# Softmax division on GpSimd and ScalarE, rotation read from PSUM, and the keys' factors on GpSimd in a four-layer encoder

## The chip, the cores and the metric

The kernel runs on one core of a Trainium2 chip. A core has a matrix engine (TensorE, PE in the profile), three engines for elementwise work (VectorE = DVE, ScalarE = ACT, GpSimd = POOL) and a queue that issues DMAs (SyncE = SP). PE, DVE and ACT can reach PSUM, the small memory into which PE writes; POOL here only works on SBUF. Each engine executes its own instructions strictly in order and waits on semaphores for the others. The metric is the time of one execution in microseconds (us); lower is better.

## The reference: what is computed

Four residual layers, `x <- x + Mixer(RMSNorm(x))`, on 512 tokens of width 1024, in float32: layer 0 and layer 3 are gated short convolutions (A), layer 1 is sparse attention (B), layer 2 is latent attention (C). All attention is softmax attention with a chunk-causal mask over 16 heads. The parts that the change touches:

```python
# B: q, k are normalised per head, then rotated
q = rope(rmsnorm(q.reshape(bsz, seq, B_HEADS, B_HEAD_DIM), q_norm), positions)
k = rope(rmsnorm(k.reshape(bsz, seq, B_HEADS, B_HEAD_DIM), k_norm), positions)
...
logits = jnp.einsum("qhd,qkhd->qhk", q_b, k_sel).astype(jnp.float32) * scale
p = jax.nn.softmax(logits, axis=-1)
return jnp.einsum("qhk,qkhd->qhd", p, v_sel)
...
# C: k is a nope part per head and a rotary part shared by all heads
k = jnp.concatenate([k_nope, jnp.broadcast_to(kr[:, :, None, :], ...)], axis=-1)
q = rmsnorm(q, q_norm)
k = rmsnorm(k, k_norm)
q = jnp.concatenate([q[..., :C_NOPE], rope(q[..., C_NOPE:], positions)], axis=-1)
```

Rotation of a vector with halves x1, x2 gives `[x1*cos - x2*sin, x2*cos + x1*sin]`. In B each query keeps only the 128 keys with the highest index scores.

## The kernel before

**Matmuls.** A float32 product is made of three passes, high*high, high*low and low*high (`products`, L272; `side_by_side`, L279). Weights come in by DMA as `raw` (L136). `convert` (L139) splits them: ACT writes the rounded high part `whi` (L153), POOL the rest `wlo = raw - whi` (L155). Four buffers each of `whi` and `wlo` stand between this and PE, so every weight that PE multiplies has passed POOL's queue.

**Order.** The program is written as Python generators, and a list scheduler with a simulated timeline fixes the order of each engine's instructions when the program is built. On the chip that order is rigid: an instruction that waits holds back all that stand behind it on its engine.

**Layer A** (`layer_a`) is eight groups of projections and an output projection, with the elementwise mixer on DVE, ACT and POOL beside it.

**Layer B** (`layer_b`). `select` (L754) computes the index scores and finds the top 128 keys with 16 rounds of MAX8 and MATCH_REPLACE8 on DVE for each of three blocks of queries. Woven into it by `weave` are `gate_steps` (gate projections `pz`, finished by `half_silu`, L409, whose first DVE instruction is `zr`, L412) and the projections of the head groups 0 and 1. `project` (L841) makes q, k and v of one group of four heads. In `query_key` (L796) ACT copies each finished PSUM bank to the tile `qk` (L802) and its squares to `qk2` (L804), DVE sums the squares (L805), POOL makes the norm factors with small instructions, among them the power (L269). Keys are multiplied by their factor on DVE (L824). Then `rotate` (L529) makes `ropea = x*C` on POOL (L534), `ropeb` = the other half times T in two DVE instructions (L538), and the sum on DVE (L540). `to_features` (L545) lets PE transpose the result through a bank (L550), and ACT and DVE write it back.

**Attention** (`attention`, L585) serves B and C. Two heads (e = 0, 1) are taken together and cut into chunks of query blocks, with 128+256, 384 and 512 keys. For a chunk `scores` runs the score matmuls, a DVE instruction that masks, scales and finds the minimum (L620), and the exponential on ACT with its sum (L623). `normalise` (L627) takes the reciprocal of the sums and multiplies p by it, both on DVE (L631, L633). `turn` transposes p on PE (L642) and copies it back (ACT L648, sometimes DVE L646), `mix` multiplies with the values (L663). Scores run four chunks ahead of `turn`, and normalise three ahead. A `Filler` puts the remaining projections between the chunks: in B groups 2 and 3, in C groups 1 to 3. These projections have two PSUM banks (tag `pj`).

**Layer C** (`layer_c`). `keys_values` (L991) makes keys and values of four heads, one block of 128 tokens at a time; POOL squares the keys (L1001), DVE sums, POOL makes the factors, and DVE multiplies the nope part and the shared rotary part with them (L1012, L1013). `queries` (L963) copies each bank (ACT L969), squares it (POOL L971), sums (DVE L972), multiplies the nope part by the gains (DVE L975), and rotates the rest. Both end in `to_features`. Before the attention starts, group 0 is projected and two gate steps run.

## Time and profile before

| | |
|---|---|
| runs before | median 1107.57 us of 3 (1105.38 to 1112.42) |
| the profiled execution | 1104.68 us, of which its span (first to last instruction of the program) is 1102.9 us |
| mean granted TensorE clock in it | 0.995 |
| instructions | 16243 |
| stages, from the timeline | layer A to about 250 us, B's index, selection and groups 0 and 1 to about 400, B's attention to about 550, C's latents to about 636, C's group 0 to about 675, C's attention to about 850, the second layer A to the end |

The profile is one execution. A "busy" share is the time in which an engine executed something. The view of groups by line gives, for all instructions of one source line, engine and shape: their count, the busy time together, the mean of one in ns, and then how long the engine stood idle just before them and what ended that idle time. The view of waits sums that idle time by waiting line and by the line it waited for. The view by windows gives, for each stretch of time, the busy time of each engine in us, with the granted clock. The timeline lists instructions with start, duration and, in brackets, the idle time before.

### The profile page before, as it was taken

How to read it: one execution, taken by the hardware profiler on the slowest of the kernel's cores; microseconds unless marked ns; L12 is line 12 of the kernel's file. 1: busy time of each engine (PE TensorE's matmuls, PEld its weight loads, DVE VectorE, ACT ScalarE, POOL GpSimd, SP SyncE). 2: the span in 40 equal slices, each digit the busy share in tenths (PEclk: the TensorE clock that was granted, in tenths of full speed). 3: DMA queues.
4: the chain of work that ended last, by engine and by line, in shares of the span. 5: the costliest groups of instructions: out<-in, count | busy, mean ns of one | idle time of the engine just before them, and what ended most of it. 6: DMA issues, size and time to landing. Idle time of an engine off the chain costs nothing.

```text
span 1102.9 us, 16243 instructions
## 1 busy us (share of the span) xinstructions
PE 1069.5 (97%) x6044; PEld 884.2 (80%) x6044; DVE 636.3 (58%) x1311; ACT 481.8 (44%) x1001; POOL 595.9 (54%) x516
## 2 busy tenths in 40 slices
PE   9999999999997989999999998999989999999998
PEld 7888888897896978888688776676767888888887
DVE  7783243346699998666723266775873474234321
ACT  6343233343443435655544445655563433232331
POOL 5655555756446665353175587263713666555552
PEclk9999999999998999999999999999999999999999
DMA  6333332323221211111022222011111333322332
GB/s 221 96 96 99 100 98 86 94 72 115 77 77 59 78 58 59 39 59 58 20 84 94 67 72 63 17 42 39 59 39 33 101 90 102 96 96 96 96 101 91
DMA packets 26575, 86.44 MB, mean 78 GB/s; under 512 B 3328, under 2 KB 4224, under 8 KB 26496
## 3 DMA queue, kind: packets, MB, share of 16 engines
q1 hardware_dynamic: 26352, 85.36, 24.4%
q8 instruction: 47, 0.77, 0.3%
q14 instruction: 32, 0.26, 0.1%
q10 hardware_dynamic: 144, 0.05, 0.0%
HBM read 83.30 MB, written 2.10 MB: 77 GB/s over the span
## 4 chain that ended last, share of the span: by engine, by line
PE 83%; DVE 11%; ACT 2%; issue 2%; DMA 1%; POOL 1%; SPq 0%; ACTq 0%; DVEq 0%; POOLq 0%
PE pa L276 10%; PE pa L275 10%; PE pa L274 10%; PE po L274 5%; PE po L275 5%; PE po L276 5%; PE o L663 4%; PE s L1038 3%; PE pt L642 3%; DVE ropeb L538 2%; PE pz L274 2%; PE pz L275 2%; PE pz L276 2%; PE tr L550 2%; PE s L283 2%
## 5 line engine op out<-in xcount | busy, mean ns | idle before, releaser
L155 POOL TENSOR_TENSOR wlo<-raw,whi 128x512 fp32r<-128x512 f32 (+4 forms) x315 | 405.2, 1293 | 329.8 <-ACT whi L153 320.8
L153 ACT ACTIVATE whi<-raw 128x512 fp32r<-128x512 f32 (+4 forms) x319 | 195.4, 616 | 366.8 <-PE pa L275 162.4
L275 PE MATMUL pa<-xl,whi 128*128 128x512 f32 x512 | 199.2, 389 | 0.0
L274 PE MATMUL pa<-xh,whi 128*128 128x512 f32 x512 | 198.6, 390 | 0.0
L276 PE MATMUL pa<-xh,wlo 128*128 128x512 f32 x512 | 197.4, 389 | 0.2 <-POOL wlo L155 0.2
L276 PEld LDWEIGHTS pa<-xh,wlo 128*128 128x128 f32 x512 | 96.0, 188 | 20.7 <-POOL wlo L155 0.6
L274 PEld LDWEIGHTS pa<-xh,whi 128*128 128x128 f32 x512 | 96.3, 188 | 20.1 <-ACT xh L346 0.2
L275 PEld LDWEIGHTS pa<-xl,whi 128*128 128x128 f32 x512 | 96.1, 188 | 19.9
L623 ACT ACTIVATE p<-p,mn 128x128 f32<-128x128 f32 (+3 forms) x128 | 71.1, 557 | 43.3 <-DVE mn L620 43.0
L447 DVE TENSOR_TENSOR cg<-pa,R 128x512 f32<-128x512 f32 x16 | 11.1, 691 | 130.2 <-PE pa L276 129.0
L663 PE MATMUL o<-pt,v 128*64 128x128 f32 x640 | 59.0, 283 | 3.6 <-ACT pt L648 2.0
L620 DVE CUSTOM_DVE_ANT_0 p<-s,cmask,qs 128x128 f32<-128x128 f32 (+2 forms) x80 | 38.2, 506 | 38.3 <-PE s L1038 31.7
L663 PEld LDWEIGHTS o<-pt,v 128*64 128x64 f32 x640 | 39.6, 136 | 19.3 <-issue 8.2
L642 PE MATMUL pt<-ident,p 128*128 128x128 f32 x320 | 50.5, 279 | 4.6 <-DVE p L633 3.3
L642 PEld LDWEIGHTS pt<-ident,p 128*128 128x128 f32 x320 | 36.4, 141 | 19.5 <-issue 13.9
L274 PE MATMUL po<-xh,whi 128*128 128x512 f32 x128 | 50.5, 394 | 1.1 <-ACT qT L111 1.1
L276 PE MATMUL pz<-xh,wlo 128*128 128x512 f32 x128 | 51.5, 403 | 0.0
L347 DVE SCALAR_TENSOR_TENSOR xl<-x,gains,xh 128x512 fp32r<-128x512 f32 x32 | 42.2, 1348 | 15.8 <-ACT xh L346 15.4
L423 DVE TENSOR_TENSOR x<-po,x 128x512 f32<-128x512 f32 x24 | 16.2, 689 | 60.6 <-PE po L276 60.6
L274 PE MATMUL pz<-xh,whi 128*128 128x512 f32 x128 | 51.0, 398 | 0.0
L275 PE MATMUL pz<-xl,whi 128*128 128x512 f32 x128 | 50.7, 396 | 0.0
L269 POOL TENSOR_TENSOR y<-mean,minus_half 128x16 f32<-128x16 f32 (+1 forms) x18 | 49.6, 2757 | 1.3
(241 smaller groups left out, 2506.7 us busy)
## 6 DMA issues: line engine op xcount, KB each, us to landing
raw<-in_a_in SPq DMA_DIRECT2D x63, 512.0 KB, 3.9
raw<-in_a_out SPq DMA_DIRECT2D x16, 512.0 KB, 3.9
raw<-in_b_z SPq DMA_DIRECT2D x8, 512.0 KB, 3.5
raw<-in_b_q SPq DMA_DIRECT2D x8, 512.0 KB, 3.4
raw<-in_b_k SPq DMA_DIRECT2D x8, 512.0 KB, 3.5
raw<-in_b_v SPq DMA_DIRECT2D x8, 512.0 KB, 3.4
raw<-in_b_out SPq DMA_DIRECT2D x8, 512.0 KB, 4.0
raw<-in_c_z SPq DMA_DIRECT2D x8, 512.0 KB, 3.6
```

The source lines that it names most:

```text
L153: act_e.activation(hi, raw[:, j:j + m], AF.Copy)
L155: e.tensor_tensor(out=lo, in0=raw[:, j:j + m], in1=hi.bitcast(F32), op=OP.subtract)
L269: pool.tensor_tensor(out=y, in0=m, in1=minus_half[:, :n], op=OP.pow)
L274: nc.tensor.matmul(o, l[0], r[0], start=first, stop=False)
L275: nc.tensor.matmul(o, l[0], r[1], start=False, stop=False)
L276: nc.tensor.matmul(o, l[1], r[0], start=False, stop=last)
L347: dve.scalar_tensor_tensor(lo, X[k], g, hi.bitcast(F32), op0=OP.mult, op1=OP.subtract)
L620: dve.tensor_tensor_reduce(out=p[:, w], in0=banks[e][:, w], in1=j["masks"](t), scale=j["qs"](e, t), scalar=-GONE, op0=OP.add, op1=OP.min, ...
L623: act_e.activation(p[:, w], p[:, w], AF.Exp, bias=mn[e][:, i:i + 1], scale=-1.0, accum_out=sm[e][:, i:i + 1])
L642: pe.transpose(b[:, i:i + P], p[:, i:i + P], ident)
L663: pe.matmul(o[64 * e:64 * e + 64, t * P:(t + 1) * P], j["v"](e, kb), x[e][:, i:i + P], start=t == 0, stop=t == NT - 1 and kb == t)
L1038: pe.matmul(o, sets[g]["q"][2 * i + e][:96, t * P:(t + 1) * P], sets[g]["k"][2 * i + e][:96, :(t + 1) * P], start=True, stop=True)
```

## The change

Four edits.

1. `normalise`: the reciprocal is taken once for both heads of a chunk pair, from one common tile of sums, and the multiplication moves from DVE: for head 0 it is a POOL tensor_scalar, for head 1 an ACT Copy with a per-partition scale.
2. `rotate` takes an optional PSUM bank. With it, the two `ropeb` instructions read the bank instead of the SBUF copy, and the final sum is on POOL instead of DVE. In B's `query_key` the rotation is now called for each bank as it is finished, ahead of the norm factors; in C's `queries` likewise.
3. The keys' factors: B's multiplication (L824 before) and C's two (L1012, L1013 before) move from DVE to POOL. In B the factor is now applied behind the rotation.
4. C's `queries`: the squares are made by ACT straight from the bank (before by POOL from the copy), ACT's copy is cut to the rotary part (4 x 32 columns instead of 384), and the nope part is multiplied by the gains on DVE straight from the bank.

The rotation of the index (idx, key) and of C's shared key keeps its old form.

```diff
-    def rotate(o, x, C, T):
+    def rotate(o, x, C, T, bank=None):
...
-            dve.tensor_tensor(pb[:, :, :, i], x[:, :, :, 1 - i],
+            dve.tensor_tensor(pb[:, :, :, i], (x if bank is None else bank)[:, :, :, 1 - i],
                                     T[:, :, None, i].to_broadcast([P, A, B, half]), op=OP.mult)
-        dve.tensor_tensor(o.rearrange("p a b i j -> p a b (i j)"), pa,
-                                pb.rearrange("p a b i j -> p a b (i j)"), op=OP.add)
+        e = dve if bank is None else pool
+        e.tensor_tensor(out=o.rearrange("p a b i j -> p a b (i j)"), in0=pa,
+                        in1=pb.rearrange("p a b i j -> p a b (i j)"), op=OP.add)
...
-            sm = [tiny("sum", n, tag="small") for _ in range(2)]
+            sm = tiny("sum", 2 * n, tag="small")
...
-                                     accum_out=sm[e][:, i:i + 1])
-                stage[c + e] = p, sm[e]
+                                     accum_out=sm[:, e * n + i:e * n + i + 1])
+                stage[c + e] = p, sm
...
         def normalise(c):
-            ts = chunks[c][2]
+            e, ts = chunks[c][1:3]
             p, sm = stage.pop(c)
-            rc = tiny("rc", len(ts), tag="small")
-            dve.reciprocal(rc, sm)
+            if e == 0:
+                rc = tiny("rc", 2 * len(ts), tag="small")
+                dve.reciprocal(rc, sm)
+                factors[c] = factors[c + 1] = rc
+            rc = factors.pop(c)[:, e * len(ts):(e + 1) * len(ts)]
             for i, (t, w) in enumerate(parts(ts)):
-                dve.tensor_scalar(p[:, w], p[:, w], rc[:, i:i + 1], None, op0=OP.mult)
+                if e == 0:
+                    pool.tensor_scalar(p[:, w], p[:, w], rc[:, i:i + 1], None, op0=OP.mult)
+                else:
+                    act_e.activation(p[:, w], p[:, w], AF.Copy, scale=rc[:, i:i + 1])
...
                 raw.append(x)
+                x5, b5 = (y.rearrange("p t (h i j) -> p t h i j", h=4, i=2)
+                          for y in (x, b.rearrange("p (t c) -> p t c", c=256)))
+                C, T = (tab[:, 2 * i:2 * i + 2] for tab in (tq if which == "q" else tk))
+                rotate(x5, x5, C, T, b5)
...
-                    dve.tensor_tensor(x3, x3, f[:, 8 * i:8 * i + 8, None].to_broadcast([P, 8, 64]), op=OP.mult)
-                x5 = x.rearrange("p t (h i j) -> p t h i j", h=4, i=2)
-                C, T = (tab[:, 2 * i:2 * i + 2] for tab in (tq if which == "q" else tk))
-                rotate(x5, x5, C, T)
+                    pool.tensor_tensor(out=x3, in0=x3, in1=f[:, 8 * i:8 * i + 8, None].to_broadcast([P, 8, 64]),
+                                       op=OP.mult)
...
-                act_e.activation(x, b[:, :384], AF.Copy)
                 q = tile_of("rp", "qk2", (P, 384))
-                pool.tensor_tensor(out=q, in0=x, in1=x, op=OP.mult)
+                act_e.activation(q, b[:, :384], AF.Square)
...
-                x = x.rearrange("p (h d) -> p h d", d=96)
-                dve.tensor_tensor(x[:, :, :64], x[:, :, :64], gqk[:, None].to_broadcast([P, 4, 64]), op=OP.mult)
-                x5 = x[:, :, 64:].rearrange("p (a h) (i j) -> p a h i j", a=1, i=2)
-                rotate(x5, x5, *(tab[:, t:t + 1] for tab in tq))
+                x, b = (y.rearrange("p (h d) -> p h d", d=96) for y in (x, b[:, :384]))
+                act_e.activation(x[:, :, 64:], b[:, :, 64:], AF.Copy)
+                dve.tensor_tensor(x[:, :, :64], b[:, :, :64], gqk[:, None].to_broadcast([P, 4, 64]), op=OP.mult)
+                x5, b5 = (y[:, :, 64:].rearrange("p (a h) (i j) -> p a h i j", a=1, i=2) for y in (x, b))
+                rotate(x5, x5, *(tab[:, t:t + 1] for tab in tq), b5)
...
-                dve.tensor_tensor(x[:, :, :64], x[:, :, :64], yt.to_broadcast([P, 4, 64]), op=OP.mult)
-                dve.tensor_tensor(x[:, :, 64:], krr[:, t, None].to_broadcast([P, 4, 32]),
-                                        yt.to_broadcast([P, 4, 32]), op=OP.mult)
+                pool.tensor_tensor(out=x[:, :, :64], in0=x[:, :, :64], in1=yt.to_broadcast([P, 4, 64]), op=OP.mult)
+                pool.tensor_tensor(out=x[:, :, 64:], in0=krr[:, t, None].to_broadcast([P, 4, 32]),
+                                   in1=yt.to_broadcast([P, 4, 32]), op=OP.mult)
```

More of the change, by code (lines that the diff above doesn't have):

```diff
@@ L595, in attention @@
                 chunks.append(c + (j["fill"][0] + (j["fill"][1] - j["fill"][0]) * (i + 1) / len(mine),))
-        stage, soft, wide, outs = {}, {}, {}, {}
+        stage, soft, wide, outs, factors = {}, {}, {}, {}, {}
         def parts(ts):
```

## The prediction

> **What bounds the kernel now.** I read the engines' shares first, then their course over time, the waits of PE, the windows of the stages that lose PE time, and the timeline around the longest wait.
>
> ```profile
> PE 1069.5 (97%) x6044; PEld 884.2 (80%) x6044; DVE 636.3 (58%) x1311; ACT 481.8 (44%) x1001; POOL 595.9 (54%) x516
> ...
> DVE  7783243346699998666723266775873474234321
> ...
> PEclk9999999999998999999999999999999999999999
> ```
>
> PE is busy 97% of the span. All that other engines can give back is the remaining 33.4 us and a little clock. DVE is full only in slices 11 to 14, some 300 to 410 us: the selection in layer B, where PEclk also dips once.
>
> ```profile
> PE pq L274 <- DVE zr L412: 5.9, 1, 5.9
> PE tr L550 <- DVE kk L1013: 3.5, 3, 1.6
> PE pt L642 <- DVE p L633: 3.3, 3, 1.5
> PE tr L550 <- DVE qk L540: 2.5, 4, 1.6
> ...
> PE pt L274 <- DVE zr L412: 1.3, 1, 1.3
> ...
> PE pt L642 <- DVE rc L631: 1.2, 1, 1.2
> ...
> PE pa L276 <- POOL wlo L155: 0.2, 1, 0.2
> ```
>
> These are PE's waits: us in total, times, longest. Nearly all that ends them is a DVE instruction that the change moves, or one that stood behind such an instruction: 17.7 us in the first six rows. POOL, by contrast, costs PE 0.2 us.
>
> ```profile
> core 0: us, PE busy (x) PEld busy (x) DVE busy (x) ACT busy (x) POOL busy (x), PEclk, DMA share, GB/s
> ...
> 325.00:350.00 25.00, 19.10 (x103) 15.69 (x102) 22.86 (x41) 7.01 (x13) 16.27 (x14) 0.86 0.24 85
> ...
> 450.00:475.00 25.00, 25.00 (x222) 21.69 (x219) 16.18 (x51) 13.84 (x38) 12.96 (x11) 1.00 0.13 43
> ...
> 650.00:675.00 25.00, 21.78 (x110) 17.25 (x109) 17.95 (x32) 12.14 (x25) 20.70 (x22) 1.00 0.20 61
> 675.00:700.00 25.00, 22.38 (x123) 17.39 (x122) 20.87 (x65) 14.47 (x38) 19.49 (x23) 0.93 0.17 51
> 700.00:725.00 25.00, 24.40 (x162) 17.20 (x161) 16.68 (x62) 18.30 (x53) 2.75 (x6) 1.00 0.00 1
> 725.00:750.00 25.00, 25.00 (x138) 20.19 (x137) 20.16 (x55) 12.23 (x30) 19.53 (x20) 1.00 0.15 46
> ```
>
> The stages differ. At 325 DVE is the limit and PE loses 5.9 us. In the middle of B's attention (450) PE is busy throughout, so that relief of DVE is worth nothing there. In C's keys (650 to 700) PE loses 5.8 us, and POOL is the busiest engine after PE: 40.2 of 50 us.
>
> ```profile
> 335.27 3.46 DVE L824 TENSOR_TENSOR qk<-qk,hf 128x512 f32<-128x512 f32 x2 [1.90 <-POOL hf L819]
> ...
> 339.12 4.15 DVE L538 TENSOR_TENSOR ropeb<-qk,table 128x256 f32<-128x256 f32 x4
> ...
> 343.72 0.67 DVE L412 SCALAR_TENSOR_TENSOR zr<-pz,R 128x512 f32<-128x512 f32 x1
> ...
> 344.45 0.58 PE L274 MATMUL pq<-whi,xh 128*128 128x256 f32 x1 [5.90 <-DVE zr L412]
> ...
> 345.47 0.41 PE L275 MATMUL pq<-wlo,xh 128*128 128x256 f32 x1
> 345.69 1.05 PE L550 MATMUL tr<-ident,qk 128*128 128x128 f32 x4
> ...
> 348.83 0.28 PE L276 MATMUL pq<-whi,xl 128*128 128x256 f32 x1
> ```
>
> This is the longest wait. DVE waits 1.90 us for the keys' factor, then applies it and rotates for 7.6 us; `zr`, which frees the bank that PE needs, stands behind. After the wait PE runs at half clock for a while (0.41 us a matmul, 0.28 later).
>
> **The change part by part.** Rows for the costs:
>
> ```profile
> L633 DVE TENSOR_SCALAR p<-p,rc 128x128 f32<-128x128 f32 (+3 forms) x128 | 49.5, 431 | 0.5
> L538 DVE TENSOR_TENSOR ropeb<-qk,table 128x256 f32<-128x256 f32 x32 | 27.5, 909 | 1.7 <-ACT qk L802 1.7
> L540 DVE TENSOR_TENSOR qk<-ropea,ropeb 128x512 f32<-128x512 f32 (+1 forms) x32 | 22.2, 695 | 0.4 <-POOL ropea L534 0.4
> L824 DVE TENSOR_TENSOR qk<-qk,hf 128x512 f32<-128x512 f32 x8 | 8.4, 1091 | 2.8 <-POOL hf L819 2.8
> L1012 DVE TENSOR_TENSOR kk<-kk,y 128x256 f32<-128x256 f32 x16 | 11.9, 741 | 0.0
> L1013 DVE TENSOR_TENSOR kk<-krr,y 128x128 f32<-128x128 f32 x16 | 10.2, 636 | 0.0
> L155 POOL TENSOR_TENSOR wlo<-raw,whi 128x512 fp32r<-128x512 f32 (+4 forms) x315 | 405.2, 1293 | 329.8 <-ACT whi L153 320.8 <-PE po L276 4.3 <-PE po L275 2.1
> L971 POOL TENSOR_TENSOR qk<-qk 128x384 f32<-128x384 f32 x16 | 13.9, 869 | 7.6 <-DVE qk L540 7.5
> L1001 POOL TENSOR_TENSOR qk<-kk 128x256 f32<-128x256 f32 x16 | 10.0, 630 | 43.5 <-ACT kk L998 41.2 <-ACT pt L648 2.0 <-DVE ropeb L538 0.3
> L534 POOL TENSOR_TENSOR ropea<-qk,ti 128x128 f32<-128x128 f32 x16 | 8.7, 544 | 0.0
> L346 ACT ACTIVATE xh<-x,gains 128x512 fp32r<-128x512 f32 x32 | 22.4, 712 | 4.4 <-DVE x L423 4.0 <-DMA x<-in_x 0.2
> L836 ACT ACTIVATE v<-pv,rtok 128x256 f32<-128x256 f32 x16 | 6.4, 474 | 5.7 <-PE pv L276 4.9 <-PE o L663 0.7
> 407.93 0.74 DVE L538 TENSOR_TENSOR ropeb<-qk,table 128x256 f32<-128x256 f32 x2
> 408.01 1.79 POOL L155 TENSOR_TENSOR wlo<-raw,whi 128x512 fp32r<-128x512 f32 x1 [3.68 <-ACT whi L153]
> ```
>
> DVE loses 49.5 (division), 22.2 (rotary sums), 8.4 and 22.1 (keys' factors): 102 us. The two `ropeb` of B take 0.37 us each when POOL rests (the 407.93 row), 0.91 on average and 1.04 in the 339.12 row. Read from PSUM I take 0.4: 32 x 0.5 = 16 us less. In all some 118 of 636 us leave.
>
> POOL gains. The division of head 0 is 64 instructions, 16 each of 128, 256, 384 and 512 elements. No POOL row has a one-input multiply of this size, so I bound it: above by two-input rows, 16 x (0.54 + 0.63 + 0.87 + 1.29) = 53 us; below by DVE's own mean, 64 x 0.43 = 28 us. I take 40, the middle, since one operand less must be read but the engine is the slower one. Sums: 16 x 1.29 + 16 x 0.54 = 29 us. Factors: 8 x 1.29 + 16 x (0.63 + 0.54) = 29 us. The squares that leave: 13.9. Net +84 (72 to 97) on 596 us. Over the whole span that fits; by stage see the second rival.
>
> ACT gains the division of head 1, 16 x (0.36 + 0.47 + 0.59 + 0.71) = 34 us (256 and 512 from rows, the others on their line), and in C 16 narrow copies of 0.36, beside the square that replaces the wide copy: 40 us on 482. Hidden: 700:725 is its fullest window here, and 6.7 of 25 us are free.
>
> No DMA is added or moved. SP's loads go on when `wlo` has consumed `raw`, so they are late only if POOL is; that belongs to the second rival.
>
> Now what lies on PE's path.
>
> 1. The 5.9 us wait and its half clock. The factor, the sums and most of `ropeb` leave DVE, so `zr` can run when its matmuls end. Gain 5.9 us, and a part of the half clock: 0.86 over 25 us means 7 us at half speed; it ended between the 345.47 and 348.83 rows, so 1.0 to 4.4 us of it were work, at a loss of half. I take 1.6 us: 7.5 us together. Late next: the POOL chain for the same keys, power, factor, two multiplies of 1.29. PE transposed these keys at 345.69 and the factor was there at 335.2, so POOL has 10 us for 2.6.
> 2. End of selection: `qk` L540 and `p` L633, 2.5 + 3.3 us. Of these I take 3.0, since the transposes then wait for POOL's sum and division instead.
> 3. C's keys: waits of 3.5 for `kk`, 1.3 for `zr` behind them, and the clock of 0.93 (1.7 us): 6.5. A group's eight factors take 4 x (0.74 + 0.64) = 5.5 us on DVE; on POOL 4 x (0.63 + 0.54) = 4.7 us, behind the power and ahead of conversions that PE needs next. I take half, 3.5.
> 4. Against it: at the ends of both attentions nothing covers the way exponential, reciprocal, division, transpose. The head-0 division now waits for both exponentials (one more ACT instruction, up to 0.7 us) and takes up to 1.29 us instead of 0.43: +0.5 each, 1 us. Inside the attentions it is hidden by the three chunks that lie between division and transpose.
> 5. Against it: banks. PE got a bank back after ACT's two reads; now DVE's `ropeb` reads it too, behind whatever stands in DVE's queue. Bounds: zero (DVE reads beside ACT), and one instruction ahead of it of the 0.7 us of L540's row for each of 32 banks, 22 us. I take 1 us, near zero, because PE was fully busy with other work in the 450 row and the long waits of DVE are what disappears.
>
> Sum: -7.5 - 3.0 - 3.5 + 1 + 1 = -12.0. From the profiled execution's 1104.68 us that is 1092.7. The median of the runs shown is 2.9 us above that execution; I add about half: 1094.
>
> The Trainium skill's page "SBUF — State Buffer", section "Who interferes with whom", says that a DVE instruction with two SBUF inputs contends with a GpSimd one that reads SBUF, one holding the other off entirely, and that a DVE instruction with at most one SBUF input doesn't. The 407.93 and 408.01 rows agree: DVE came first and kept 0.37 us, POOL took 1.79 instead of 1.29. By that rule the reads from PSUM cost 0.4 us however busy POOL is, as I took.
>
> **The rivals.**
>
> *Hidden anyway* (chance 0.24). The scheduler lays out all queues anew, and every wait that goes is replaced by another. For it: in the 450 row PE is full already, and for none of the 17.7 us does the trace show what would be late next. Against it: the 5.9 us wait has one evident cause. Gain 0 to 5 us: 1100 to 1108.
>
> *POOL becomes the bound in C* (chance 0.18), ending on the other side. In 650:700 POOL has 40.2 of 50 us. Two groups add 2 x 4.7 (factors) + 8 x 0.54 (sums) - 8 x 0.87 (squares) = 6.7, and the first pair's division up to 3.3: 50.2 of 50. C's attention, 675 to 850, has eight pairs of heads, so 25 us carry up to 3.8 us of division: in 725:750 that makes 19.5 + 4.7 + 2.2 - 3.5 + 3.8 = 26.7 of 25, and I take the last group as alike. As PE takes all weights through POOL, each overrun, with the 9.8 and 5.5 us in which POOL now idles for its inputs, falls on PE: up to 10 + 2 x 7.2 = 24 us, less the 7.5 of step 1: 1123 with the same 1.3 on top; at half of the 24, 1111. It decides when PE's waits for `wlo`, now 0.2 us, pass 12 us. Against it: with 28 instead of 53 us for the division the overruns vanish, and in 700:725 POOL has room. The Trainium skill's "GPSIMD Engine Reference", section "Engine selection", advises against elementwise work on GpSimd: two-input work about half VectorE's speed, one input near line rate. The 1.29 us for 512 elements agrees with the first; for the second no run here has a row.
>
> *All of it goes* (chance 0.1). The six rows' 17.7 us with both clock dips, and shorter bubbles around them: 22 to 26 us, 1080 to 1085.
>
> **How the numbers follow.** The forecast has 0.48, its own range 1087 to 1101. About 1% (11 us) is what a measurement tells from no change: faster means under 1096.5, slower over 1118.6. Seven tenths of the forecast and all of the third rival lie under it: 0.34 + 0.10 = 0.44. Of the POOL case somewhat over half lies above: 0.10. The rest, 0.46, is within 1%. The range leaves out half of the last rival and a good half of the POOL case, 0.15 in all: 1083 to 1116.
>
> **What would show it.** Right: no wait of several us at `zr` near 340, PEclk without a dip there; L538 near 0.4 us; POOL near 680 us and DVE near 520. Step 3 is right if `kk` waits shrink without waits for `wlo`. Wrong: PE waiting for POOL's p, kk, qk or `wlo`, POOL's one-input multiply above 1.3 us for 512 elements, or PE waiting on banks for `ropeb`.

## The result, and the profile after

| | before | after |
|---|---|---|
| median of the runs compared (us) | 1109.2 (1105.38 to 1112.42) | 1082.38 (1082.1 to 1082.77) |
| ratio after / before | | 0.976, 95% interval 0.9725 to 0.9794 |
| profiled execution (us) / its span | 1104.68 / 1102.9 | 1082.3 / 1080.5 |
| mean granted clock in it | 0.995 | 0.999 |

The change makes the kernel 2.4% faster, 22.4 us between the two profiled executions, where the prediction had 12.0. The medians differ by 26.8: the profiled execution of before was faster than each of the four. Both numbers are used below, each beside its own kind: medians with medians, profiles with profiles.

The page of after, engines and their course:

```profile
PE 1061.9 (98%) x6044; PEld 881.5 (82%) x6044; DVE 520.4 (48%) x1063; ACT 514.0 (48%) x1081; POOL 693.3 (64%) x636
...
DVE  7784234345588964444423244443552463344221
...
POOL 5656555666387898586375589695934765555552
PEclk9999999999999999999999999999999999999999
```

DVE is full in one slice instead of four, the dip of PEclk at slice 12 is gone, and POOL has gained 97 us and is full in four slices. PE's own balance: its idle time in the span fell from 33.4 to 18.6 us, and the busy time of the same 6044 matmuls by 7.6. PE's waits after, in us in total, times, longest:

```profile
PE pt L274 <- DVE ropeb L539: 1.9, 2, 1.2
PE pt L651 <- ACT pt L657: 1.8, 4, 0.9
PE tr L552 <- DVE key L746: 1.5, 1, 1.5
PE o L672 <- ACT pt L657: 1.4, 4, 0.7
...
PE pt L651 <- POOL p L640: 0.9, 2, 0.5
...
PE pz L276 <- POOL wlo L155: 0.4, 1, 0.4
...
PE pa L276 <- POOL wlo L155: 0.3, 1, 0.3
```

All six rows of 17.7 us are gone, and nothing of their size stands in their place. The windows of after at two of the stages discussed, and at POOL's fullest (columns as in the prediction):

```profile
325.00:350.00 25.00, 25.00 (x164) 21.55 (x163) 22.23 (x46) 10.36 (x19) 18.92 (x16) 1.00 0.24 85
375.00:400.00 25.00, 24.60 (x204) 22.42 (x202) 18.66 (x49) 15.49 (x38) 24.66 (x24) 1.00 0.26 85
650.00:675.00 25.00, 23.69 (x133) 19.32 (x131) 10.52 (x36) 18.64 (x49) 24.29 (x33) 1.00 0.17 53
675.00:700.00 25.00, 23.98 (x179) 18.13 (x178) 11.40 (x43) 20.46 (x56) 17.78 (x21) 1.00 0.15 43
```

At 325 PE runs 164 matmuls where it ran 103. POOL is 97 to 99% busy in the second and third rows, and PE still waits for `wlo` only 0.7 us in the whole run.

Where the 22.4 us come from is read off the timelines, at marks that every variant has: the last DVE instruction of the selection that makes a mask, the first matmul of C's latents (the end of B), and the end of the program. In the profiles:

| | selection done | end of B | end |
|---|---|---|---|
| before | 412.19 | 590.39 | 1102.89 |
| after, less before | -16.82 | -11.98 | -22.42 |

So B gives 12.0 us and C 10.4. The prediction's own terms are -9.0 for B (steps 1 and 2, half of 4, and 5) and -3.0 for C. The -16.8 at the mask isn't all gain: the window of after from 300 us to there holds 733 matmuls,

```profile
300.00:395.40 95.40, 95.00 (x733) 88.05 (x733) 84.66 (x202) 45.61 (x93) 81.03 (x69) 1.00 0.24 80
```

where that of before (shown below) holds 770. Some work has moved behind the mask: from there to the end of B, after takes 183.0 us where before took 178.2. A part of these 4.8 us has another cause, the split division, which is taken up below.

### The profile page after: what moved, and what is told of

It reads as the page before. It is cut to its first block, busy times and chain, and to the rows that moved or that the text cites. A ratio compares the mean times of both kernels' runs of the same rounds, so it can differ in the third digit from the quotient of the medians.

```text
span 1080.5 us, 16178 instructions
## 1 busy us (share of the span) xinstructions
PE 1061.9 (98%) x6044; PEld 881.5 (82%) x6044; DVE 520.4 (48%) x1063; ACT 514.0 (48%) x1081; POOL 693.3 (64%) x636
## 4 chain that ended last, share of the span: by engine, by line
PE 91%; DVE 3%; ACT 3%; issue 1%; POOL 1%; DMA 1%; SPq 0%; DVEq 0%; POOLq 0%; ACTq 0%
PE pa L276 10%; PE pa L275 10%; PE pa L274 10%; PE po L274 5%; PE po L275 5%; PE po L276 5%; PE o L672 4%; PE pt L651 3%; PE s L1049 3%; PE pz L276 2%; PE pz L274 2%; PE pz L275 2%; PE tr L552 2%; PE s L283 2%; PE pk L274 2%; PE pq L274 2%
## 5 line engine op out<-in xcount | busy, mean ns | idle before, releaser
L640 POOL TENSOR_SCALAR p<-p,rc 128x128 f32<-128x128 f32 (+1 forms) x64 | 70.3, 1105 | 55.4 <-DVE rc L635 50.1
L672 PE MATMUL o<-pt,v 128*64 128x128 f32 x640 | 56.6, 283 | 1.8 <-ACT pt L657 1.4
L275 PE MATMUL po<-xl,whi 128*128 128x512 f32 x128 | 50.3, 393 | 0.0
L275 PE MATMUL po<-glo,whi 128*128 128x512 f32 x128 | 49.8, 389 | 0.0
```

The lines of the kernel that those rows point to most:

```text
L275: nc.tensor.matmul(o, l[0], r[1], start=False, stop=False)
L640: pool.tensor_scalar(p[:, w], p[:, w], rc[:, i:i + 1], None, op0=OP.mult)
L672: pe.matmul(o[64 * e:64 * e + 64, t * P:(t + 1) * P], j["v"](e, kb), x[e][:, i:i + P], start=t == 0, stop=t == NT - 1 and kb == t)
```

## The experiments

The prediction's theory was that `zr` is freed because the keys' factor and the sums leave DVE. Its rival is that the rotation does it: asked for at each bank and not behind the factor, and read from the bank. Times are medians; ratios are to runs of before taken beside them.

### Each edit alone

`only_division` has edit 1, `only_rotation` edits 2 and 4 (with the key's factor still on DVE), `only_factors` edit 3. Cores of the three diffs against before, in this order:

```diff
-                dve.tensor_scalar(p[:, w], p[:, w], rc[:, i:i + 1], None, op0=OP.mult)
+                if e == 0:
+                    pool.tensor_scalar(p[:, w], p[:, w], rc[:, i:i + 1], None, op0=OP.mult)
+                else:
+                    act_e.activation(p[:, w], p[:, w], AF.Copy, scale=rc[:, i:i + 1])
...
-            dve.tensor_tensor(pb[:, :, :, i], x[:, :, :, 1 - i],
+            dve.tensor_tensor(pb[:, :, :, i], (x if bank is None else bank)[:, :, :, 1 - i],
...
+        e = dve if bank is None else pool
...
-                    dve.tensor_tensor(x3, x3, f[:, 8 * i:8 * i + 8, None].to_broadcast([P, 8, 64]), op=OP.mult)
+                    pool.tensor_tensor(out=x3, in0=x3, in1=f[:, 8 * i:8 * i + 8, None].to_broadcast([P, 8, 64]),
+                                       op=OP.mult)
```

> Edit 1 alone on the kernel before. Theory A (each edit gives what it takes from DVE in the stage where DVE was late): selection in B hardly moves (mask finished at 412 us before, 395 after; here 409 to 412), and the 5.9 us wait of PE for zr stays, since the keys' factor and ropeb still stand ahead of it on DVE; B's attention neutral or 2 us longer; C's attention, from its first score matmul to its last value matmul, falls from 168.4 us to about 163, since a chunk's division no longer stands between other DVE work. Total 5 to 8 us faster than before. Rival B (the division only moved a wait to POOL, whose one-input multiply takes 1.57 us for 512 elements): C's attention stays at 167 to 170 us and the total within 3 us of before.

> Edits 2 and 4 alone on the kernel before (rotation from the bank with its sum on POOL, C's squares on ACT; division and keys' factors stay on DVE). Theory A: the two ropeb pairs of 0.9 us become 0.41 and run early, so the selection ends 6 to 10 us earlier than before (412.2 us), and the 5.9 us wait shrinks, though the factor of 2 x 1.1 us or more and its wait for POOL stay ahead of zr. C's keys and attention change by less than 2 us, since kk stays on DVE. Total 7 to 11 us faster. Rival B (any one part that thins DVE's queue takes away the same long wait): 12 us or more in the selection alone, so that the parts add up to much more than the whole.

> Edit 3 alone on the kernel before (keys' factors of B and C on POOL; rotation and division stay on DVE). Theory A: DVE no longer waits for the factor with zr behind it, so the 5.9 us wait and the half clock go (7.5 us), and C's waits for kk (3.5 us, of which 2.3 in its attention's first 25 us) go too: 3 us in C. Selection ends at about 404 us. Total 8 to 12 us faster. Rival B (the factor on POOL delays the rotation behind it, ropea being on POOL too, and the conversions): selection gains under 4 us and the total is under 5 us.

| | us | ratio (95%) |
|---|---|---|
| only_division | 1102.06 | 0.9942 (0.9923 to 0.9961) |
| only_rotation | 1081.68 | 0.9764 (0.9736 to 0.9792) |
| only_factors | 1109.37 | 1.0013 (0.9996 to 1.003) |

The rotation alone is as fast as the whole change, where 7 to 11 us were expected of it. The factors alone, on which step 1 was built, do nothing, where 8 to 12 us were expected. Only the division came out about as expected. The DVE timeline of `only_factors` at the long wait says why:

```profile
338.29 2.65 DVE L538 TENSOR_TENSOR ropeb<-qk,table 128x256 f32<-128x256 f32 x2 [2.43 <-POOL qk L824]
...
341.40 2.35 DVE L538 TENSOR_TENSOR ropeb<-qk,table 128x256 f32<-128x256 f32 x2
343.68 0.68 DVE L412 SCALAR_TENSOR_TENSOR zr<-pz,R 128x512 f32<-128x512 f32 x1
```

DVE no longer multiplies by the factor, but it stands for 2.43 us until POOL has, because the rotation is still behind the factor; and `zr`, behind the rotation, starts at 343.68, where before it was 343.72. PE's wait stays:

```profile
PE pq L274 <- DVE zr L412: 5.1, 1, 5.1
```

In `only_rotation`, where DVE still multiplies:

```profile
335.74 0.69 DVE L412 SCALAR_TENSOR_TENSOR zr<-pz,R 128x512 f32<-128x512 f32 x1 [2.25 <-PE pz L276]
...
338.26 2.37 DVE L830 TENSOR_TENSOR qk<-qk,hf 128x512 f32<-128x512 f32 x2
```

`zr` now waits for its own matmuls and runs as soon as they end; the factor comes after it. What freed `zr` is that the rotation left the place between the factor and `zr`, not that the factor left DVE. `early_from_copy`, in the next section, is the plain test of this.

### The rotation, place by place and step by step

`rotation_in_b` makes the rotation's edit in B's `query_key` only, `rotation_in_c` in C's `queries` only (with edit 4). `early_from_copy` only moves the call in B: at each bank, ahead of the factors, but still from the SBUF copy with the sum on DVE. `early_from_bank` adds the read from the bank and leaves the sum on DVE. The last step of the ladder, the sum on POOL, is `rotation_in_b`. The diff of `early_from_copy`, and what the other adds to it:

```diff
                 raw.append(x)
+                x5 = x.rearrange("p t (h i j) -> p t h i j", h=4, i=2)
+                C, T = (tab[:, 2 * i:2 * i + 2] for tab in (tq if which == "q" else tk))
+                rotate(x5, x5, C, T)
...
-                x5 = x.rearrange("p t (h i j) -> p t h i j", h=4, i=2)
-                C, T = (tab[:, 2 * i:2 * i + 2] for tab in (tq if which == "q" else tk))
-                rotate(x5, x5, C, T)
...
+                rotate(x5, x5, C, T, b5)
```

> Edit 2 in B's query_key alone (rotation per finished bank, read from the bank, sum on POOL); C as before. Theory A (the gain of the rotation is of two places, 14.5 us in B and 7.8 us in C, as the kernel with the rotation alone had them at the same marks): first output projection of B 14 us earlier than before (529.0 us), C's stages as long as before, total 12 to 16 us faster. Rival B (one long wait less in B also puts the rest of the program into a better order): over 18 us.

> Edits 2 and 4 in C's queries alone (bank read by ropeb and by the gains, squares on ACT, sum on POOL); B as before. Theory A: B unchanged within 1 us, the 5.9 us wait stays, C's group 0 about 2 us and C's attention about 6 us shorter, total 6 to 9 us faster. Rival B: C's gain came from B's changed order and clock; total within 3 us of before.

> Order alone: in B's query_key the rotation is called for each bank as it is finished, ahead of the keys' factor, but reads the SBUF copy and sums on DVE as before. Theory A1 (the wait of 5.9 us came of the order: ropeb could not start before the factor): the wait goes with DVE's work unchanged, selection ends 2 to 5 us earlier, total 6 to 9 us faster. Theory A2 (DVE is full in the selection, and only work taken from it counts): selection ends within 2 us of before, total under 4 us faster.

> As the order alone, and ropeb reads the bank, but the sum stays on DVE. A1: 2 to 3 us faster than the order alone. A2: ropeb at 0.41 instead of 0.91 us takes 8 us from DVE in the selection, which ends 6 to 9 us earlier than before; total 7 to 10 us faster, and the sums on POOL make up the rest to 14 us.

Times, and the marks of the profiles less those of before:

| | us | ratio (95%) | selection done | end of B | end |
|---|---|---|---|---|---|
| early_from_copy | 1099.91 | 0.9921 (0.9897 to 0.9946) | -5.4 | -4.2 | -3.4 |
| early_from_bank | 1098.95 | 0.9909 (0.9881 to 0.9936) | -11.7 | -9.3 | -4.6 |
| rotation_in_b | 1091.71 | 0.9845 (0.9818 to 0.9872) | -14.2 | -15.5 | -12.5 |
| rotation_in_c | 1098.92 | 0.9906 (0.9875 to 0.9936) | +1.5 | +3.8 | -4.1 |
| only_rotation | 1081.68 | 0.9764 (0.9736 to 0.9792) | -13.2 | -14.5 | -22.3 |

The marks have an error of their own: `rotation_in_c` leaves B as it was, yet its B ends 3.8 us later (its profile has one more half-clock stretch there). Differences under some 4 us in one mark are not read. With that, the order alone is a part, about 5 us at the end of the selection, the bank adds about 6, and the sum on POOL 2.5, which is within the error there and 6 at the end of B. In whole-run medians the bank without the sum is not told from the order alone (the intervals overlap), and the sum is. The two places together make the whole: by the ratios 17 us for B, 10 for C, 26 for both. In B this is edit 2 alone. In C it is edits 2 and 4 together, which no run separates, so how much of the 10 us is the rotation and how much the squares and copies of edit 4 stays open.

In `early_from_copy` the factor, the sum and the read of the SBUF copy are all still on DVE, and the wait of 5.9 us for `zr` is gone from PE's waits. `zr` now stands ahead of the factor:

```profile
337.49 0.67 DVE L412 SCALAR_TENSOR_TENSOR zr<-pz,R 128x512 f32<-128x512 f32 x1
...
339.63 2.34 DVE L827 TENSOR_TENSOR qk<-qk,hf 128x512 f32<-128x512 f32 x2 [0.94 <-POOL hf L822]
```

So the order is enough for this wait, as theory A1 had it. A2 has its share too: with the bank the selection ends another 6 us earlier, beyond its 6 to 9. The order alone also makes DVE's work shorter, though no instruction left: the 32 `ropeb` take 0.67 us on average instead of 0.91. One of them takes about 0.41 us, or up to 1.52 while a POOL instruction runs; at the earlier place 6 of them take over 1.4 us, before it was 12.

Why it goes on after the longest wait has gone is seen in DVE's own sum of work in the selection. Windows from 300 us to the end of the selection, of before, `only_rotation`, `early_from_copy` and `ropeb_twice` (next section), whose columns are as in the prediction:

```profile
300.00:412.20 112.20, 101.49 (x770) 92.86 (x769) 107.85 (x225) 45.27 (x92) 66.77 (x56) 0.97 0.22 71
```

```profile
300.00:399.00 99.00, 99.00 (x774) 92.02 (x773) 91.21 (x213) 44.92 (x92) 75.39 (x66) 1.00 0.25 81
```

```profile
300.00:406.77 106.77, 100.92 (x769) 91.91 (x768) 102.92 (x226) 44.62 (x92) 66.16 (x56) 1.00 0.23 75
```

```profile
300.00:403.00 103.00, 99.18 (x753) 91.09 (x752) 99.24 (x233) 44.09 (x90) 73.89 (x65) 0.98 0.23 77
```

Before, DVE was busy 107.85 of 112.2 us, 96%: the stage was as long as DVE's list. With the rotation's edit 16.6 us leave that list, the stage is 13.2 us shorter for nearly the same number of matmuls, and PE becomes the full engine, 99.00 of 99.00. In between the stage goes with DVE's busy time: in before, `early_from_copy`, `early_from_bank` (100.45 us, DVE 95.98) and `ropeb_twice` it is 3.8 to 4.5 us longer than that.

### Giving DVE its work back: ropeb_twice

This is `only_rotation` with each `ropeb` that reads a bank computed twice into the same place.

```diff
         for i in range(2):
-            dve.tensor_tensor(pb[:, :, :, i], (x if bank is None else bank)[:, :, :, 1 - i],
-                                    T[:, :, None, i].to_broadcast([P, A, B, half]), op=OP.mult)
+            for _ in range(1 if bank is None else 2):
+                dve.tensor_tensor(pb[:, :, :, i], (x if bank is None else bank)[:, :, :, 1 - i],
+                                        T[:, :, None, i].to_broadcast([P, A, B, half]), op=OP.mult)
```

> The kernel with the rotation alone, and each ropeb that reads a bank is made twice, with the same result: 32 more DVE instructions of 0.41 us in B, 16 of them in the selection (6.6 us), and 32 of 0.21 in C. Theory (the selection lasts as long as DVE's work in it): selection ends 5 to 7 us later than with the rotation alone (399.0 us), total 5 to 9 us above 1081.7. Rival (a single wait was removed and DVE has slack now): selection ends within 2 us, total within 2 us.

1096.2 us, ratio 0.9884 (0.9857 to 0.991): of the 26 us, 13 (by the ratios) to 14.5 (by the medians) are given back, more than the 5 to 9 expected. The groups of 16, 16 and 32 instructions became 32, 32 and 64 of the same durations (0.41, 0.41 and 0.22 us): 19.3 us more of DVE's list, 8.2 of it (20 instructions) in the selection. There the stage, from the index's first transpose to the mask, grows from 136.0 to 141.3 us. PE's waits now begin with

```profile
PE tr L553 <- DVE kk L1017: 3.8, 2, 2.6
PE pk L274 <- DVE ropeb L540: 2.7, 1, 2.7
```

and half clock is back in three stretches of 13.7 us in all, one of 3.4 at the end of the selection and two in C ahead of its attention. No wait for `zr` is back, and yet the selection is longer: work put on DVE's list where the list is full comes back as time. The scheduler has laid the queues out anew here too, so the order isn't quite that of `only_rotation`. How much of the 5.3 us is the list's sum, how much the bank held longer (the second row, 2.7) and how much the half clock (at most 1.7), this run can't separate. Of the 13.6 us between the two profiles' ends, 7.0 arise behind B, of which the two stretches in C explain at most 5.1; the rest is not traced.

### Leaving one part out of the whole

`no_factors` and `no_division` are after with that one edit undone. `head0_dve` puts only head 0's division back on DVE. `pool_broadcast` keeps it on POOL in another form.

```diff
-                    pool.tensor_tensor(out=x3, in0=x3, in1=f[:, 8 * i:8 * i + 8, None].to_broadcast([P, 8, 64]),
-                                       op=OP.mult)
+                    dve.tensor_tensor(x3, x3, f[:, 8 * i:8 * i + 8, None].to_broadcast([P, 8, 64]), op=OP.mult)
...
-                if e == 0:
-                    pool.tensor_scalar(p[:, w], p[:, w], rc[:, i:i + 1], None, op0=OP.mult)
-                else:
-                    act_e.activation(p[:, w], p[:, w], AF.Copy, scale=rc[:, i:i + 1])
+                dve.tensor_scalar(p[:, w], p[:, w], rc[:, i:i + 1], None, op0=OP.mult)
...
-                    pool.tensor_scalar(p[:, w], p[:, w], rc[:, i:i + 1], None, op0=OP.mult)
+                    dve.tensor_scalar(p[:, w], p[:, w], rc[:, i:i + 1], None, op0=OP.mult)
...
-                    pool.tensor_scalar(p[:, w], p[:, w], rc[:, i:i + 1], None, op0=OP.mult)
+                    pool.tensor_tensor(out=p[:, w], in0=p[:, w], in1=rc[:, i:i + 1].to_broadcast([P, w.stop - w.start]),
+                                       op=OP.mult)
```

> The changed kernel with the keys' factors back on DVE (division and rotation as changed). Theory (the rotation carries the gain; factors and division are worth nothing beside it): within 3 us of the changed kernel's 1082.4 us. Rival (the parts need each other: with the rotation there, DVE becomes free enough only when the factors leave too): 1086 us or more, with waits of PE for kk of 2 us or more in C.

> The changed kernel with the division back on DVE (rotation and factors as changed). Theory (the division costs 2.5 us at the end of B's attention, as it did alone, and gives some back in C's attention): within 3 us of 1082.4, B's way from its first output projection to the first matmul of C's latents back at 61.4 us instead of 63.9. Rival (the division was needed for C's attention): C's attention 164 us or more instead of 159.9, total 1085 or more.

> The changed kernel with head 0's division on DVE and head 1's on ACT (nothing of the division on POOL). Theory (the POOL division is what lengthens the uncovered end of B's attention by 2.5 us): that stretch, first output projection to first matmul of C's latents, goes from 63.9 to about 61.5 us, total 1079 to 1081 us, faster than both kernels. Rival (the end is long because head 0 waits for both heads' sums, whatever engine divides): stretch unchanged, total within 1 us of 1082.4.

> The changed kernel with POOL's division as a tensor_tensor of p and the factor broadcast along the row, instead of a tensor_scalar. Theory (POOL's two-input form takes 1.29 us for 512 elements where tensor_scalar took 1.57, so the form costs, not a lock by DVE): 128 to 512 elements in 0.5 to 1.35 us, 64 of them 58 us or less instead of 70; total 0 to 2 us faster than 1082.4. Rival (both forms run at the same rate when POOL has the port): still 66 us or more, time unchanged.

| | us | ratio (95%) | selection done | end of B | end |
|---|---|---|---|---|---|
| no_factors | 1087.73 | 0.9815 (0.9793 to 0.9836) | -13.9 | -11.6 | -15.2 |
| no_division | 1089.86 | 0.9835 (0.9816 to 0.9855) | -15.6 | -8.9 | -14.9 |
| head0_dve | 1087.34 | 0.9813 (0.9793 to 0.9833) | -16.6 | -9.1 | -17.4 |
| pool_broadcast | 1081.92 | 0.976 (0.9741 to 0.9779) | -17.2 | -13.9 | -22.1 |

The parts do not add, and the first theory on record failed for three of the four: `no_factors` and `no_division` were expected within 3 us of after and `head0_dve` ahead of it, and they are 5.0 to 7.5 us slower. Beside the rotation, the factors alone cost 8.2 us (`no_division` against `only_rotation`), the division alone 6.1 (`no_factors` against it), and both together 0.7, which is no difference by the intervals. For one of these losses a cause is in the trace. (In `no_factors` PE also waits 2.4 us for `kk` on DVE, which after doesn't, and 3.4 us at half clock are back at 683 us.) In `no_division`, PE and DVE at the end of the selection:

```profile
393.90 0.36 PE L274 MATMUL pk<-whi,xh 128*128 128x256 f32 x1 [2.47 <-DVE ropeb L539]
```

```profile
385.10 2.51 DVE L635 TENSOR_SCALAR p<-p,rc 128x128 f32<-128x128 f32 x3
...
393.01 0.74 DVE L539 TENSOR_TENSOR ropeb<-pq,table 128x256 f32<-128x256 f32 x2
```

The bank is held until `ropeb` has read it, and `ropeb` stands on a DVE list to which the division has come back (three instructions, 2.51 us) between the rounds of the selection; from 385.10 on that list is full. That is the mechanism of step 5, in a kernel where DVE is full again. The rest of these losses is not traced to rows.

Step 4's place is seen alike in all of them. From B's first output projection (`po`) to C's latents PE runs 61.4 us without the split division in B (before, `only_rotation`, `no_division`), and 63.9 with it (after, `only_division`, `no_factors`): 2.5 us. Five more matmuls lie in the stretch then, 358 for 353, which make PE 0.7 us busier; the other 1.8 us are PE's waits, 2.8 us in after for 0.8 in before. `head0_dve` tests whether POOL's slow instruction is the cause, and has 64.1 with waits of 2.8 us, 2.1 of them for DVE's division instead, so POOL alone isn't the cause; `pool_broadcast` has 63.3. The remaining candidates, the reciprocal that waits for both heads' sums and head 1's step on ACT, were not separated.

### The best version: rotation everywhere, the rest only in C

In B the rotation alone ends at -14.5 us and the whole change at -12.0; in C's attention the whole change is the shorter one. Windows of C's attention, of before, `only_rotation` and after:

```profile
674.50:842.90 168.40, 158.44 (x987) 118.82 (x985) 121.02 (x365) 99.11 (x257) 74.40 (x80) 0.99 0.12 37
```

```profile
658.00:820.60 162.60, 157.11 (x993) 119.06 (x991) 108.25 (x352) 102.25 (x272) 67.73 (x79) 1.00 0.13 38
```

```profile
660.60:820.50 159.90, 154.18 (x987) 117.35 (x985) 74.21 (x241) 114.71 (x301) 111.74 (x136) 1.00 0.13 39
```

168.4, 162.6 and 159.9 us. Both differences between the last two kernels are under the error of a mark; the runs that join the better halves are the test. `rest_in_c` therefore takes the rotation in B and C, and the division's split and the factors on POOL in C only; `rest_in_c_broadcast` does the same with POOL's other form.

```diff
+            split = chunks[c][0].get("split")
+            if split is None:
+                rc = tiny("rc", len(ts), tag="small")
+                dve.reciprocal(rc, sm)
+            elif e == 0:
+                rc = tiny("rc", 2 * len(ts), tag="small")
+                dve.reciprocal(rc, sm)
+                factors[c] = factors[c + 1] = rc
...
+                if split is None:
+                    dve.tensor_scalar(p[:, w], p[:, w], rc[:, i:i + 1], None, op0=OP.mult)
+                elif e == 0:
+                    pool.tensor_scalar(p[:, w], p[:, w], rc[:, i:i + 1], None, op0=OP.mult)
+                else:
+                    act_e.activation(p[:, w], p[:, w], AF.Copy, scale=rc[:, i:i + 1])
```

> Rotation in B and C; division split over POOL and ACT, and keys' factors on POOL, in C alone; in B division and factors stay on DVE. Theory (the stages add: B as with the rotation alone, 14.5 us earlier at the first matmul of C's latents; C's latents and attention as in the changed kernel, 10.4 us shorter than before): span about 1078, time 1078 to 1080 us, faster than both. Rival (C's 8.5 us depend on how the schedule happened to fall): C's attention 161 to 163 us, total within 1 us of 1081.7.

> As rest_in_c, with POOL's division as a tensor_tensor with the factor broadcast (1.04 instead of 1.57 us for 512 elements). Theory: as rest_in_c or up to 2 us faster, 1077 to 1080 us, since the uncovered end of C's attention has one division less by 0.5 us. Rival: C's attention 162 us as in the changed kernel with this form, total 1081 or more.

`rest_in_c`: 1079.18 us (1078.99 to 1079.55), ratio 0.9733 (0.9709 to 0.9757); `rest_in_c_broadcast`: 1080.32 us, 0.9743 (0.9719 to 0.9768). The first has the lowest median of all kernels run, 3.2 us under after's. The two were not run beside each other, and the intervals of their ratios overlap (0.9709 to 0.9757, and 0.9725 to 0.9794); no execution of either reaches the other's range. Its marks are -15.7 at the end of B and -26.2 at the end: B gives what the rotation alone gives, C gives 10.5.

```profile
PE 1060.1 (98%) x6044; PEld 880.9 (82%) x6044; DVE 555.8 (52%) x1159; ACT 498.8 (46%) x1049; POOL 649.7 (60%) x596
```

DVE has 35 us more to do than in after, and the kernel is faster: in B, with the rotation moved, unloading DVE further buys nothing.

## Why the prediction was wrong

It had the sign and the rows of the waits right. The size was about half of what came: 12.0 us for 22.4 between profiles, and after's median, 1082.38, lies 0.6 us below the stated range of 1083 to 1116. Two of its three gains were credited to the wrong edits. The step that failed most is step 3.

- **Step 1 (-7.5).** The place and the size of the wait were right: 5.9 us and the clock dip are gone. The reason, "the factor, the sums and most of `ropeb` leave DVE", failed: `only_factors` leaves the wait at 5.1 us, and `early_from_copy` removes it with all three still on DVE. It is the order that decides: the rotation no longer stands behind the factor and ahead of `zr`. That edit 2 makes this move as well is why the wait went all the same: the term came out right by luck.
- **Step 2 (-3.0).** Steps 1 and 2 together were -10.5 for the selection; the mask comes 16.8 us earlier, some of it for work moved behind it, and the end of B gains 12.0 against -9.0. Half of the named waits was held back for what would be late next. Nothing of that size was: with 16.6 us off a DVE list that was 96% full (`only_rotation`), PE itself became the full engine. The step priced PE's waits one by one where the stage's length was DVE's sum; the windows from 300 us give it.
- **Step 3 (-3.5, at the factors).** This is the term that was most mis-sized: C gives 10.4 us, against -3.0 with its half of step 4. (Half of its 6.5 us is 3.25; 3.5 was taken.) And the part it named does nothing by itself: of C's attention, 168.4 us long, edits 2 and 4 (`rotation_in_c`) take off 5.8 us and bring the wait for `kk` from 3.5 to 1.4 with the factors still on DVE, the division alone (`only_division`) takes off 6.0, the factors alone add 0.4. Beside the other two the factors do count (`no_factors` 166.3, after 159.9). A stage's length in one profile is uncertain by about 3 us (in `rotation_in_b`, which leaves C as it was, it is 171.5, with 10.2 us at half clock), so the shares are no finer than that. DVE's list in C's attention fell from 121.0 to 74.2 us, of which the prediction counted only what ended a named wait. Of the 8.5 us, 4.2 are PE's idle time (168.40 - 158.44 less 159.90 - 154.18) and the rest is in the busy time of an equal number of matmuls, of which the 3.4 us at half clock at 689 explain at most 1.7. The remainder stays open.
- **Step 4 (+1).** Right in sign, too small: 2.5 us at the end of B alone, where half of 1 was taken. That POOL's slower division makes it is not borne out (`head0_dve`).
- **Step 5 (+1).** In after there is hardly a wait of this kind, 1.9 us for `pt` behind `ropeb` (1.2 us of it stands in `only_rotation` too). The mechanism is real where DVE is full (`no_division` 2.5, `ropeb_twice` 2.7). The read from the bank costs 0.41 us, as taken. (The 0.37 us that the prediction reads off the 407.93 row halves two instructions that overlap; each takes 0.41.)
- **Work moved.** DVE 520.4 (forecast 520), POOL 693.3 (680), ACT +32 (+40). The bound of 28 to 53 us for POOL's division did not hold: it is 70.3 us. The bound from above rested on the assumption that an instruction with one tile less to read can't be slower than a two-input one; here it is.
- **Rivals.** "Hidden anyway" fell. "All of it goes" is what took place, at 0.1: all six rows and both dips are gone, and its 22 to 26 us hold the 22.4. Its sum fits in part by luck: PE's idle time fell by 14.8 us, less than the 17.7 of the rows, and of the 7.6 us less of busy time the two dips explain at most 3.3 (half of the 3.2 us of work in the first and of the 3.4 in the second). "POOL becomes the bound in C" fell: it was to decide at 12 us of waits for `wlo`, and there are 0.7, though POOL is as full in C's keys as it forecast (49.1 of the 50 us from 638 us, for 50.2); in C's attention it is busy 111.7 of 159.9 us. So POOL at 97 to 99% cost PE here 0.7 us for `wlo` and 0.9 for its division.
- **The base.** The 1.3 us added for the median were not needed: after's median is its profiled execution's time to 0.1 us. Before has a spread of 7 us and changing half-clock dips; kernels without dips in their profile (after, `only_rotation`, `rest_in_c`, `head0_dve`) have 0.6 to 1.1. That is a correlation only: `only_factors` has two dips and a spread of 1.0, `rest_in_c_broadcast` no dip and 1.9.

## What to carry to other kernels

Look at each stage by itself. In the selection PE idled and DVE was busy 96% of the time, and the stage's length went with DVE's list: price a change in such a stage by the work that leaves the list, and take the waits that PE shows for its symptoms. Before crediting a removed instruction with a wait, look at what stands between it and the late one: here moving a dependent step out from between removed the wait, and moving the producer to another engine did not.

Apply each part only where it can pay. DVE's share alone doesn't tell: in before it was busy 71% of the time from the mask to B's first output projection, and 72% in C's attention. But PE was busy 116.50 of 116.83 us in the first, and the split division brought only its cost, 2.5 us at the end of that attention. In C's attention PE idled 10.0 us, and with the division and the factors added there `rest_in_c` is 2.5 us ahead of `only_rotation` by the medians.

## What the runs showed of the hardware

**A one-input multiply on POOL is slower than a two-input one.** Rows by form, first of after, then of `pool_broadcast`, where the factor is read as a second tensor of one repeated element:

```profile
L640 POOL TENSOR_SCALAR p<-p,rc 128x512 f32<-128x512 f32 x16 | 25.1, 1566 | 15.8 <-DVE rc L635 15.6
L542 POOL TENSOR_TENSOR qk<-ropea,ropeb 128x512 f32<-128x512 f32 x16 | 20.9, 1306 | 2.0 <-DVE ropeb L539 1.6 <-PE pk L276 0.4
...
L640 POOL TENSOR_SCALAR p<-p,rc 128x128 f32<-128x128 f32 x16 | 9.7, 609 | 29.6 <-DVE rc L635 28.3 <-PE pt L651 1.2
```

```profile
L640 POOL TENSOR_TENSOR p<-p,rc 128x512 f32<-128x512 f32 x16 | 16.7, 1041 | 22.2 <-DVE rc L635 22.0
...
L640 POOL TENSOR_TENSOR p<-p,rc 128x128 f32<-128x128 f32 x16 | 6.4, 401 | 34.7 <-DVE rc L635 34.5
```

1566 ns for 512 elements with a per-partition factor, 1306 for two full inputs, 1041 with the repeated factor. The Trainium skill's "GPSIMD Engine Reference", section "Engine selection", has one-input work at nearly line rate; these rows differ (DVE took 0.58 us for the same 512 elements in before), and the measurement decides. The saving of 23 us of POOL time (70.3 to 47.1) moved the run by 0.5 us, inside the spread.

**Reading one operand from PSUM takes `ropeb` out of POOL's way.** The mean of 0.91 us became 0.41, though POOL has more to do than before. The trace of before points to POOL: the 6 of the 32 beside which no POOL instruction of over 0.3 us ran took 0.41 us each, and of the other 26, 18 took 0.65 to 1.52. In after none of the 32 takes more than 0.43. Durations in before (least, median, most, in ns), then the row by form of after:

```profile
L538 DVE TENSOR_TENSOR ropeb<-qk,table x32: 409/842/1523, 294.9 to 500.6; 128x256 f32<-128x256 f32 x32
```

```profile
L539 DVE TENSOR_TENSOR ropeb<-pq,table 128x256 f32<-128x256 f32 x16 | 5.9, 412 | 0.3 <-ACT qk L813 0.3
```

**PE's clock fell after an idle time of 1.6 us.** The timeline of before in C, and the windows around it:

```profile
687.88 0.31 PE L550 MATMUL tr<-ident,kk 128*96 128x128 f32 x1 [1.59 <-DVE kk L1013]
```

```profile
687.40:690.80 3.40, 2.92 (x10) 1.90 (x11) 3.40 (x10) 1.78 (x5) 1.51 (x3) 0.72 0.77 269
690.80:694.20 3.40, 3.40 (x11) 2.00 (x11) 3.40 (x14) 1.54 (x3) 1.29 (x2) 0.77 0.03 11
```

The half-clock stretch begins near 688.9 and lasts 3.4 us; those inside the other profiles last 3.4, 6.8 or 10.2. The Trainium skill's page "TensorE: Matmul & The Clock Gate", section "Why this matters for your kernels", asks for no idle gaps above about 3 us; here a shorter one stood ahead of the dip. One case doesn't give a threshold: after has an idle time of 1.5 us (`key`, above) and no dip.
